# Layer 1's channel mixer on single PSUM banks, with an early copy of the first half product

## The chip, the cores and the metric

One NeuronCore of a Trainium2 chip runs one whole inference step of a small decoder. The metric is the time of one execution on the device in microseconds; before the change it is 2571.55 us, the median of three runs (2570.28 to 2572.80). Names of engines as in the profile: PE (TensorE matmul) and PEld (its weight loads), DVE (VectorE), ACT (ScalarE), POOL (GpSimd), SP (SyncE, which issues the DMAs). L521 is line 521 of the kernel.

## What is computed

Two layers over 1024 prompt tokens and 64 sample tokens, 1024 channels each. After every token mixer comes a channel mixer of 2816 hidden channels; the change touches layer 1's.

```python
def swiglu(h, w_in, w_out):
    g, u = jnp.split(h @ w_in, 2, axis=-1)
    return (jax.nn.silu(g) * u) @ w_out
...
        for layer in range(DEPTH):
            ...
            h = h + mix
            h = h + swiglu(rms_norm(h, norm_ffn_g[layer]), w_ffn_in[layer], w_ffn_out[layer])
        y = rms_norm(h, norm_final_g)
```

## The kernel before

**Data and groups.** Activations lie transposed, channels on partitions and tokens on the free axis. The 1088 tokens are two groups: GA, tokens 0 to 511, and GB, the 576 others. Layer 1's channel mixer runs first for GA, then for GB (`channel1`, which calls `run_ffn`).

**Precision.** Each float32 matmul is three matmuls of split operands: ACT casts a weight or activation to its high part, POOL (for weights, L186 and L197) or DVE (for activations, L241) subtracts to get the low part. Weights arrive by DMA into `stage` tiles (four buffers), and `w_split` turns them into `hl` tiles (three buffers). `w_next` takes the next `hl` tile, and splits two tiles ahead of it; so the call stands in the program where that work enters the queues of DVE, ACT and POOL. Every engine works off its queue in program order (the schedule is written by hand).

**Seven products for eight.** A block f of 128 hidden channels needs a gate part and an up part, each of 1024 input channels over the group's tokens. `strassen(f)` forms both from seven half products (half of the input channels by half of the tokens, 12 matmuls each) with sums of the weights and of the activations. The activations' sums (t1 to t4, b11, b21, b22) are formed once per group. The weights' sums are formed anew for every f on DVE: L200, L201 and L202 (`sum512`, and the two halves of `sum1024`) ahead of an f, L214 (`sum_c`) within it. The products are, in order: two halves of X, two of Y (the second is the "fourth product"), two of Z, and W. In the profile, "b" and "x" name the activation sums: an f is 36 matmuls on x, 12 on b, 12 on x, 24 on b, and the last 12 of these are W.

**From products to the gate.** ACT copies Y's second half into G (L537), since DVE adds one PSUM operand to one SBUF operand. DVE then adds: U's first half is X's first half plus G; U's second half is X's second half plus U's first; two sums of Y's first half go to P and G; three more take Z and W (all L525, seven per f). Then SiLU on ACT (L550), the gating product on POOL (L500) and the split for the next stage (L240 on ACT, L241 on DVE), the latter two deferred by `post`, `late` and `flush`.

**Order and stages.** The f are taken in pairs; after each pair but the first, the out blocks of the pair before follow: 8 blocks of 128 output channels, 12 matmuls each, added to the residual by DVE (L295). So the sums for an odd f enter DVE's queue in the even f, in the `w_next` that belongs to Z, ahead of that f's adds; the sums for the next even f are interleaved with the out blocks (`thin`). GA's last two pairs' out blocks come together at its end (`out_both`), where DVE also builds GB's operands. GB's f 0 is computed plainly.

**PSUM.** `accs()` takes a tile from a pool of three tiles of two banks each (`acc_pool(GB, 3)`), for both groups; two more banks serve small matmuls. In GA every tile but X, Y and Z uses half of its space. A tile is given out again when all readers of its last use are done. Hence W takes the tile that X had. Layer 0's second group uses `strassen` too, with `done` false (its activations aren't normalised beforehand in the same way); in layer 1 `done` is true.

Of the kernel before, what the change touches and what calls it, by code (L numbers as in the profile page):

```python
# [11 lines left out]
AF = mybir.ActivationFunctionType  # L12
# [33 lines left out]
GA = Grp(0, HALF, (0, 1, 512, 0))  # L46
GB = Grp(HALF, T, (0, 2, 288, 0))
# [10 lines left out]
def trunk_kernel(ctx, tc, x_prompt, x_sample, cache_k, cache_v, state_conformer, state_shortconv, state_pool,  # L58
# [4 lines left out]
    pe, act, dve, pool, sp = nc.tensor, nc.scalar, nc.vector, nc.gpsimd, nc.sync  # L63
# [12 lines left out]
    tmpbox = [gstack.enter_context(tc.tile_pool(name="tmpg", bufs=4, side="right")), 640]  # L76

    def tmp():
        return tmpbox[0].tile([128, tmpbox[1]], F, name="tmp")
# [89 lines left out]
    def need(upto):  # L169
        a, b, _ = seq[min(upto, len(seq)) - 1]  # L170
        return max(a, b or 0) + 1
# [50 lines left out]
    def w_next(live=0):  # L222
        j = wj[0]
        wj[0] += 1
        w_split(j + 3 - live)
        w_load(need(j + 6 - live))
        return hls.pop(j)
# [228 lines left out]
    def run_ffn(g, accs, ps, hidp, x, last, sig=False, slot=lambda: None, forms=None, plain=NF,  # L456
                free=lambda: None, hw=None, both=True):
        G = NF // 2
        n = g.n
        hid = {}  # L460
        gate = {}
        done = forms and "switch" not in forms

        def ev_g(a):
            t = tmp()
            if done:
                for p, o in parts(g, a, t):
                    act.activation(o, p, AF.Silu)
                gate["t"] = t
                return  # L470
            scaled(g, t[:, :n], a)
            if sig:
                s = tmp()
                act.activation(s[:, :n], t[:, :n], AF.Sigmoid)
                pool.tensor_tensor(t[:, :n], t[:, :n], s[:, :n], op=OP.mult)
            else:
                act.activation(t[:, :n], t[:, :n], AF.Silu)  # L477
            gate["t"] = t

        def to_hid(f):  # L480
            if f // 2 not in hid:
                hid[f // 2] = hidp.tile([128, 2, 2, hw or n], FR, name="hid")[:, :, :, :n]
            return hid[f // 2][:, f % 2]

        def ev_u(f, a):
            if done:
                t, dst = gate.pop("t"), to_hid(f)
                for p, o in parts(g, a, t):
                    dve.tensor_tensor(o, p, o, op=OP.mult)
                late.append(lambda: split(dst, t[:, :n]))  # L490
                return
            t = tmp()
            scaled(g, t[:, :n], a)
            gated(f, t, gate.pop("t"))

        def gated(f, t, u):
            dst = to_hid(f)

            def fin():
                (dve if both and f == NF - 1 else pool).tensor_tensor(t[:, :n], t[:, :n], u[:, :n], op=OP.mult)  # L500
                late.append(lambda: split(dst, t[:, :n]))
            post.append(fin)

        def one(f, which):
            h = w_next()
            a = accs()
            block(g, a, h, x, K0[4:] + K0[:4] if done else K0, slot=slot)
            flush()
            ev_g(a) if which == 0 else ev_u(f, a)
            slot()  # L510

        def strassen(f):
            w2 = n // 2

            def prod(acc, h, i, b):
                for k in range(4):
                    xk = forms[b](k)
                    for s, (wi, xi) in enumerate(((0, 0), (0, 1), (1, 0))):  # L520
                        pe.matmul(acc[:, :w2], h[:, wi, i, k], xk[:, xi], start=k == 0 and s == 0,  # L521
                                  stop=k == 3 and s == 2)

            def add(out, acc, x):
                dve.tensor_tensor(out, acc[:, :w2], x, op=OP.add)  # L525

            a, b = slice(0, w2), slice(w2, n)
            X, h = accs(), w_next()
            prod(X[:, 0], h, 0, "t2")
            prod(X[:, 1], h, 1, "t3")  # L530
            flush()
            slot()
            Y, h = accs(), w_next()
            prod(Y[:, 0], h, 0, "t1")
            prod(Y[:, 1], h, 1, "b11")
            G_, U, P = tmp(), tmp(), tmp()
            act.activation(G_[:, a], Y[:, 1, :w2], AF.Copy)  # L537
            Z, h = accs(), w_next()
            prod(Z[:, 0], h, 0, "t4")
            add(U[:, a], X[:, 0], G_[:, a])  # L540
            add(U[:, b], X[:, 1], U[:, a])
            add(P[:, b], Y[:, 0], U[:, b])
            add(G_[:, b], Y[:, 0], U[:, a])
            prod(Z[:, 1], h, 1, "b21")
            W, h = accs(), w_next()
            prod(W[:, 0], h, 0, "b22")
            add(P[:, a], Z[:, 0], U[:, b])
            add(G_[:, a], Z[:, 1], G_[:, a])
            add(G_[:, b], W[:, 0], G_[:, b])
            act.activation(G_[:, :n], G_[:, :n], AF.Silu)  # L550
            gated(f, P, G_)
            slot()

        for q in range(G + 1):
            if q < G:
                for f in (2 * q, 2 * q + 1):
                    if f >= plain:
                        if f == plain:
                            forms.get("switch", forms.get("ready"))()
                        strassen(f)  # L560
                        continue
                    if f == 0 and not done:
                        run_in(g, accs, x, [ev_g, lambda a: ev_u(0, a)], norm_hooks(g, ps, at=(4, 7)), skew=3)
                        slot()
                        continue
                    one(f, 0)
                    one(f, 1)
            if q == G - 1:
                free()
                if both:  # L570
                    return last([hid.pop(q - 1), hid.pop(q)])
            if q == G:
                flush()
                flush()
                last(hid.pop(q - 1))
            elif q:
                hh = hid.pop(q - 1)
                for o in range(2):
                    thin[0] = True
                    h = w_next()  # L580
                    thin[0] = False
                    for i in range(4):
                        a = accs()
                        out_block(g, a, h, i, hh)
                        added(g, hb[:, o * 4 + i, g.cs], a)
                        if parts_:
                            parts_.pop(0)()
                        if o == 0 and i == 1:
                            flush()
                        slot()  # L590
# [40 lines left out]
    def acc_pool(g, bufs):  # L631
        accstack.close()
        accbox["p"] = accstack.enter_context(tc.tile_pool(name=f"acc{g.c0}_{g.n}", bufs=bufs, space=PSUM))
        accbox["g"] = g

    def accs():
        return accbox["p"].tile([128, len(accbox["g"].blocks), 512], F, name="acc")
# [1087 lines left out]
    for n in range(2, KC):  # L1725
        h = w_next()
        a = accs()
# [4 lines left out]
    with tc.tile_pool(name="fab", bufs=1) as ep:  # L1732
        gen = forms_a(ep)
        for n in range(KC):
            h = w_next()
            a = accs()
# [8 lines left out]
    ystack0 = ExitStack()  # L1745
    tstack.close()
    r1stack.close()
    fp = fstack.enter_context(tc.tile_pool(name="forms1", bufs=1))
    tmpbox[:] = [ystack0.enter_context(tc.tile_pool(name="tmph", bufs=4, side="right")), 640]
    hidp1 = ystack0.enter_context(tc.tile_pool(name="hid1", bufs=2, side="right"))  # L1750
    xs = [fp.tile([128, 2 * GB.n], F, name=f"xs{k}") for k in range(4)]
    L, R = slice(0, W2), slice(W2, GB.n)
# [63 lines left out]
    def channel1(g, last, side, free, plain, x):  # L1816
        side = side()
        turn[0] = 0
        j0 = wj[0]

        def slot():
            turn[0] += 1
            if seam:
                return go_on()
            if jobs and g is GB:
                if turn[0] % 3 == 0:
                    jobs.pop(0)()
            elif turn[0] % 3 == 0:
                if g is GA or wj[0] > j0 + 2 * plain + 2:
                    next(side, 0)  # L1830

        def end(hh):
            if g is GB:
                for _ in side:
                    pass
                fstack.close()
            last(hh)

        run_ffn(g, accs, ms, hidp1, x, end, slot=slot, forms=dict(form_views(g.n // 2), ready=ready), plain=plain,
                free=free, hw=GB.n, both=g is GA)  # L1840
# [9 lines left out]
    def rows_a():  # L1850
# [11 lines left out]
        for t in range(4):  # L1862
            for i in range(2):
# [5 lines left out]
                sp.dma_start(y_p[0, t * 128:t * 128 + 128, 512 * i:512 * i + 512], y)  # L1869
                yield 1  # L1870

    channel1(GA, last_a1, forms_b, free_a, PLAIN1[0], None)


    ystack = ExitStack()
# [117 lines left out]
```

## Time and profile before

| | |
|---|---|
| median of three runs | 2571.55 us |
| the profiled execution | 2568.46 us |
| its span, first to last instruction | 2566.7 us |
| mean granted TensorE clock | 0.991 |
| GA's channel mixer of layer 1, about | 1774 to 2151 us of the span |
| GB's, without the final rows, about | 2151 to 2522 us |
| L537, copies of the fourth product | 60, 383 to 414 ns |
| L525, adds from PSUM | 420, 409 to 460 ns |

A row of the timeline reads: start, duration, engine, line, operation, output tile <- input tiles, shapes, how many were merged, and in brackets the idle time of the engine just before and what ended it. A row of waits reads: who waited, for whom, microseconds in all, how many times, the longest. A row of the stretches reads: its ends, its length, then the busy time of PE, PEld, DVE, ACT and POOL with the number of instructions, the granted clock, the DMA share and GB/s. Merged rows overlap where instructions are pipelined, so that a duration over a count is a little more than one's spacing.

### The profile page before, as it was taken

Reading aid. Unit: us, or ns where it says so; the run is one execution under the profiler, and the core shown is the slowest. Engines: PE = TensorE matmul, PEld = TensorE weight load, DVE = VectorE, ACT = ScalarE, POOL = GpSimd, SP = SyncE. Lnnn points to the kernel's source line nnn. Section 1 sums busy time; section 2 is a strip of 40 time slices with the busy share of each in tenths; the row PEclk is TensorE's granted clock in tenths of the full one; section 3 lists DMA queues with packets and bytes.
Section 4 is the critical chain, followed back from the end, with each engine's and each line's share of the span. In section 5 each row is a group of like instructions: output and inputs, shape, how many; then the busy total and the mean of one; then the engine's idle time right before and its main releaser. Section 6 shows DMA issues by size and latency. Waiting matters only on the chain.

```text
span 2566.7 us, 41423 instructions
## 1 busy us (share of the span) xinstructions
PE 2467.6 (96%) x15871; PEld 2196.0 (86%) x15871; DVE 1695.6 (66%) x2359; ACT 1106.1 (43%) x1875; POOL 1562.3 (61%) x1201
## 2 busy tenths in 40 slices
PE   8999999999999989999999999999999999999998
PEld 6788876777777768989999889989888888999997
DVE  3696767867878844567656633348777778666655
ACT  4536766754444334334333521234433444443333
POOL 6754234434443346678777722266888886887775
PEclk9999999999999999999999999999999999999999
DMA  7342231225455534222323411152323332333322
GB/s 220 114 113 74 65 105 50 62 66 158 143 171 166 148 108 156 70 74 83 99 83 99 129 42 42 44 158 61 92 85 97 99 99 83 107 95 103 99 84 79
DMA packets 355485, 258.31 MB, mean 101 GB/s; under 512 B 22913, under 2 KB 303617, under 8 KB 355272
## 3 DMA queue, kind: packets, MB, share of 16 engines
q1 hardware_dynamic: 355256, 255.66, 33.9%
q8 instruction: 126, 2.06, 0.3%
q14 instruction: 71, 0.58, 0.1%
q10 hardware_dynamic: 32, 0.01, 0.0%
HBM read 237.41 MB, written 18.69 MB: 100 GB/s over the span
## 4 chain that ended last, share of the span: by engine, by line
PE 45%; DVE 8%; POOL 2%; issue 1%; ACT 1%; POOLq 0%; DVEq 0%; ACTq 0%
PE acc L235 24%; PE acc L521 20%; POOL hl L197 1%; DVE hid L241 1%; DVE sum L200 1%; DVE sum L201 1%; DVE hb L295 1%; DVE b L1673 0%; DVE tmp L525 0%; DVE sum_c L214 0%; DVE sum L202 0%; DVE fb L1677 0%; PE blk L1896 0%; DVE x L1673 0%; POOL tmp L500 0%
## 5 line engine op out<-in xcount | busy, mean ns | idle before, releaser
L186 POOL TENSOR_TENSOR hl<-stage,hl 128x512 fp32r<-128x512 f32 x464 | 638.1, 1399 | 461.1 <-ACT hl L184 336.4
L235 PE MATMUL acc<-x,hl 128*128 128x512 f32 (+1 forms) x3648 | 788.4, 354 | 12.6 <-DVE hb L295 2.6
L235 PEld LDWEIGHTS acc<-x,hl 128*128 128x128 f32 x3648 | 584.8, 191 | 84.6 <-issue 14.1
L235 PE MATMUL acc<-hid,hl 128*128 128x288 f32 (+1 forms) x3096 | 551.3, 334 | 18.5 <-DVE hb L295 8.9
L235 PEld LDWEIGHTS acc<-hid,hl 128*128 128x128 f32 x3096 | 471.5, 190 | 72.4 <-DVE hb L295 13.0
L295 DVE TENSOR_TENSOR hb<-acc,hb 128x512 f32<-128x512 f32 (+1 forms) x360 | 256.1, 718 | 177.2 <-PE acc L235 175.8
L521 PE MATMUL acc<-x,hl 128*128 128x288 f32 (+1 forms) x2676 | 362.8, 291 | 4.7 <-POOL hl L197 1.9
L521 PEld LDWEIGHTS acc<-x,hl 128*128 128x128 f32 x2676 | 349.4, 189 | 7.1 <-POOL hl L197 2.7
L184 ACT ACTIVATE hl<-stage 128x1024 fp32r<-128x1024 f32 x232 | 243.6, 1055 | 224.0 <-PE acc L235 139.9
L197 POOL TENSOR_TENSOR hl<-sum,hl 128x512 fp32r<-128x512 f32 x180 | 237.1, 1345 | 168.5 <-ACT hl L196 168.5
L525 DVE TENSOR_TENSOR tmp<-acc,tmp 128x288 f32<-128x288 f32 (+1 forms) x420 | 173.5, 441 | 228.2 <-ACT tmp L537 135.4
L197 POOL TENSOR_TENSOR hl<-stage,hl 128x512 fp32r<-128x512 f32 x180 | 267.1, 1505 | 13.3 <-ACT hl L196 13.3
L521 PE MATMUL acc<-b,hl 128*128 128x256 f32 (+1 forms) x1548 | 216.6, 291 | 13.2 <-DVE tmp L525 10.3
L521 PEld LDWEIGHTS acc<-b,hl 128*128 128x128 f32 x1548 | 202.3, 190 | 18.8 <-ACT hl L196 8.5
L235 PE MATMUL acc<-x1t,hl 128*128 128x288 f32 x1152 | 216.4, 296 | 1.5 <-POOL hl L186 1.5
L235 PEld LDWEIGHTS acc<-x1t,hl 128*128 128x128 f32 x1152 | 196.1, 189 | 19.4 <-POOL hl L186 1.7
L196 ACT ACTIVATE hl<-sum 128x512 fp32r<-128x512 f32 x180 | 103.1, 623 | 237.2 <-DVE sum L202 212.3
L291 DVE TENSOR_TENSOR tmp<-acc,rr 128x512 f32<-128x512 f32 (+1 forms) x108 | 75.1, 709 | 111.1 <-PE acc L235 99.1
L500 POOL TENSOR_TENSOR tmp<-tmp 128x576 f32<-128x576 f32 (+1 forms) x85 | 127.6, 1501 | 16.3 <-ACT tmp L477 8.3
L196 ACT ACTIVATE hl<-stage 128x512 fp32r<-128x512 f32 x180 | 105.6, 618 | 67.3 <-PE acc L235 62.0
L241 DVE TENSOR_TENSOR hid<-tmp,hid 128x512 fp32r<-128x512 f32 (+1 forms) x88 | 100.0, 1138 | 48.1 <-ACT hid L240 47.8
L235 PE MATMUL acc<-x1a,hl 128*128 128x512 f32 x480 | 122.4, 409 | 3.0 <-POOL hl L186 1.3
(287 smaller groups left out, 3162.4 us busy)
## 6 DMA issues: line engine op xcount, KB each, us to landing
stage<-in_w_ffn_in_dram SPq DMA_DIRECT2D x176, 512.0 KB
stage<-in_w_ffn_out_dram SPq DMA_DIRECT2D x88, 512.0 KB
stage<-in_w_in_even_dram SPq DMA_DIRECT2D x40, 512.0 KB
kst<-in_cache_k_dram SPq DMA_DIRECT2D x64, 256.0 KB
vst<-in_cache_v_dram SPq DMA_DIRECT2D x64, 256.0 KB
stage<-in_w_out_even_dram SPq DMA_DIRECT2D x16, 512.0 KB
stage<-in_w_in_odd_dram SPq DMA_DIRECT2D x16, 512.0 KB
stage<-in_w_out_odd_dram SPq DMA_DIRECT2D x16, 512.0 KB
```

Of the source, the lines that this page charges most:

```text
L184: act.activation(hl[:, 0], st, AF.Copy)
L186: pool.tensor_tensor(hl[:, 1, c], st[:, c], f32(hl[:, 0, c]), op=OP.subtract)
L196: act.activation(hl[:, 0, c], x, AF.Copy)
L197: pool.tensor_tensor(hl[:, 1, c], x, f32(hl[:, 0, c]), op=OP.subtract)
L200: todo = [lambda: dve.tensor_tensor(sb, su[:, lo], su[:, hi], op=OP.add), lambda: dve.tensor_tensor(sa[:, hi], sg[:, lo], su[:, lo], op=OP ...
L235: pe.matmul(acc[:, b, :c1 - c0], w, xs[:, xi, c0 - o:c1 - o], start=first and s == 0, stop=last and s == 2)
L241: (on or dve).tensor_tensor(dst[:, 1], src, f32(dst[:, 0]), op=OP.subtract)
L291: dve.tensor_tensor(d, a, r, op=OP.mult)
L295: dve.tensor_tensor(d, a, d, op=OP.add)
L500: (dve if both and f == NF - 1 else pool).tensor_tensor(t[:, :n], t[:, :n], u[:, :n], op=OP.mult)
L521: pe.matmul(acc[:, :w2], h[:, wi, i, k], xk[:, xi], start=k == 0 and s == 0, stop=k == 3 and s == 2)
L525: dve.tensor_tensor(out, acc[:, :w2], x, op=OP.add)
```

## The change

In GA's layer 1 the pool becomes six tiles of one bank each (`acc_pool(GA, 6)`), and goes back to three pairs for GB. `bank()` hands out halves of a tile, so GB still works on pairs. In layer 1 (`done`) ACT copies X's first half into U right after that product, and the first add becomes Y's second half plus U, in place, placed right after the fourth product and so ahead of the `w_next` of Z. The copy of Y's second half into G stays, as G's first half is still needed later. The pool of temporaries gets a fifth buffer, as U is taken earlier.

```diff
+            box = []
+            def bank():
+                if not box:
+                    t = accs()
+                    box.extend(t[:, i] for i in range(t.shape[1]))
+                return box.pop(0)
...
-            X, h = accs(), w_next()
-            prod(X[:, 0], h, 0, "t2")
-            prod(X[:, 1], h, 1, "t3")
+            h = w_next()
+            X = bank(), bank()
+            prod(X[0], h, 0, "t2")
+            if done:
+                U = tmp()
+                act.activation(U[:, a], X[0][:, :w2], AF.Copy)
+            prod(X[1], h, 1, "t3")
             flush()
             slot()
...
-            prod(Y[:, 1], h, 1, "b11")
-            G_, U, P = tmp(), tmp(), tmp()
-            act.activation(G_[:, a], Y[:, 1, :w2], AF.Copy)
-            Z, h = accs(), w_next()
-            prod(Z[:, 0], h, 0, "t4")
-            add(U[:, a], X[:, 0], G_[:, a])
-            add(U[:, b], X[:, 1], U[:, a])
+            prod(Y[1], h, 1, "b11")
+            if done:
+                add(U[:, a], Y[1], U[:, a])
+            G_ = tmp()
+            act.activation(G_[:, a], Y[1][:, :w2], AF.Copy)
...
+            h = w_next()
+            Z = [bank()]
+            prod(Z[0], h, 0, "t4")
+            if not done:
+                add(U[:, a], X[0], G_[:, a])
+            add(U[:, b], X[1], U[:, a])
...
-            W, h = accs(), w_next()
-            prod(W[:, 0], h, 0, "b22")
+            h = w_next()
+            W = bank()
+            prod(W, h, 0, "b22")
...
-    tmpbox[:] = [ystack0.enter_context(tc.tile_pool(name="tmph", bufs=4, side="right")), 640]
+    tmpbox[:] = [ystack0.enter_context(tc.tile_pool(name="tmph", bufs=5, side="right")), 640]
...
+    acc_pool(GA, 6)
     channel1(GA, last_a1, forms_b, free_a, PLAIN1[0], None)
+    acc_pool(GB, 3)
```

How the queues change is best seen in one even f of GA, on DVE. Before (the rows from `sum_c` to the next `sum_c`; tile numbers follow the names, acc_19400 is X and acc_19434 is Y):

```order
L214 TENSOR_TENSOR sum_c_19402<-stage_19228,sum1024_19315 128x512 [waits DVE_49,Pool_49]
L241 TENSOR_TENSOR hid_19188<-tmp_19258,hid_19188 128x512 [waits Activation_49]
L200 TENSOR_TENSOR sum512_19469<-stage_19366 128x512 [waits DMAHW3_49,Pool_49]
L201 TENSOR_TENSOR sum1024_19468<-stage_19364,stage_19366 128x512 [waits DMAHW2_49,DVE_49]
L202 TENSOR_TENSOR sum1024_19468<-sum512_19469,stage_19364 128x512 [waits DVE_49]
L525 TENSOR_TENSOR tmp_19463<-acc_19400,tmp_19462 128x256 [waits Activation_49]
L525 TENSOR_TENSOR tmp_19463<-acc_19400,tmp_19463 128x256 [waits DVE_49]
L525 TENSOR_TENSOR tmp_19464<-acc_19434,tmp_19463 128x256 [waits DVE_49,PE_49]
```

And after (acc_19485 is the bank of Y's second half, acc_19452 that of X's second):

```order
L214 TENSOR_TENSOR sum_c_19445<-stage_19270,sum1024_19359 128x512 [waits DVE_49,Pool_49]
L241 TENSOR_TENSOR hid_19228<-tmp_19303,hid_19228 128x512 [waits Activation_49]
L525 TENSOR_TENSOR tmp_19465<-acc_19485,tmp_19465 128x256 [waits PE_49]
L200 TENSOR_TENSOR sum512_19516<-stage_19410 128x512 [waits DMAHW3_49,Pool_49]
L201 TENSOR_TENSOR sum1024_19515<-stage_19408,stage_19410 128x512 [waits DMAHW2_49,DVE_49]
L202 TENSOR_TENSOR sum1024_19515<-sum512_19516,stage_19408 128x512 [waits DVE_49]
L525 TENSOR_TENSOR tmp_19465<-acc_19452,tmp_19465 128x256
```

One add has moved ahead of the three sums and waits for PE alone, that is for the fourth product; the sums stand behind it.

On ACT, the same f before, from the hid cast to the cast of the sums:

```order
L240 ACTIVATE hid_19188<-tmp_19258 128x512 [waits Pool_49]
L196 ACTIVATE hl_19435<-sum_c_19402 128x512 [waits DVE_49,PE_49,Pool_49]
L537 ACTIVATE tmp_19462<-acc_19434 128x256 [waits PE_49]
L196 ACTIVATE hl_19467<-sum1024_19468 128x512 [waits DVE_49,Pool_49]
```

And after, where L541 is the new copy and L552 what was L537:

```order
L541 ACTIVATE tmp_19465<-acc_19451 128x256 [waits PE_49]
L240 ACTIVATE hid_19228<-tmp_19303 128x512 [waits Pool_49]
L196 ACTIVATE hl_19481<-sum_c_19445 128x512 [waits DVE_49,PE_49,Pool_49]
L552 ACTIVATE tmp_19511<-acc_19485 128x256 [waits DVE_49]
L196 ACTIVATE hl_19514<-sum1024_19515 128x512 [waits DVE_49,PE_49,Pool_49]
```

The new copy stands ahead of the hid cast, and the copy of the fourth product now waits for DVE (the add that reads the same bank) instead of PE.

On PE, the first matmul of W before (a tile of two banks) and after (one bank):

```order
L521 MATMUL acc_19505<-b2_0_16849,hl_19435 128x256 [waits DVE_49,Activation_49]
...
L521 MATMUL acc_19560<-b2_0_16849,hl_19481 128x256 [waits Activation_49]
```

W no longer waits for DVE there.

More of the change, by code (lines that the diff above doesn't have):

```diff
@@ L527, in strassen @@
             a, b = slice(0, w2), slice(w2, n)
-            X, h = accs(), w_next()
-            prod(X[:, 0], h, 0, "t2")
-            prod(X[:, 1], h, 1, "t3")
+            box = []
[11 more added lines that the diff above has]
+            prod(X[1], h, 1, "t3")
             flush()
             slot()
-            Y, h = accs(), w_next()
-            prod(Y[:, 0], h, 0, "t1")
-            prod(Y[:, 1], h, 1, "b11")
-            G_, U, P = tmp(), tmp(), tmp()
-            act.activation(G_[:, a], Y[:, 1, :w2], AF.Copy)
-            Z, h = accs(), w_next()
-            prod(Z[:, 0], h, 0, "t4")
-            add(U[:, a], X[:, 0], G_[:, a])
-            add(U[:, b], X[:, 1], U[:, a])
-            add(P[:, b], Y[:, 0], U[:, b])
-            add(G_[:, b], Y[:, 0], U[:, a])
-            prod(Z[:, 1], h, 1, "b21")
-            W, h = accs(), w_next()
-            prod(W[:, 0], h, 0, "b22")
-            add(P[:, a], Z[:, 0], U[:, b])
-            add(G_[:, a], Z[:, 1], G_[:, a])
-            add(G_[:, b], W[:, 0], G_[:, b])
+            h = w_next()
+            Y = bank(), bank()
+            prod(Y[0], h, 0, "t1")
+            prod(Y[1], h, 1, "b11")
[4 more added lines that the diff above has]
+            if not done:
+                U = tmp()
+            P = tmp()
+            h = w_next()
+            Z = [bank()]
+            prod(Z[0], h, 0, "t4")
+            if not done:
+                add(U[:, a], X[0], G_[:, a])
+            add(U[:, b], X[1], U[:, a])
+            add(P[:, b], Y[0], U[:, b])
+            add(G_[:, b], Y[0], U[:, a])
+            Z.append(bank())
+            prod(Z[1], h, 1, "b21")
+            h = w_next()
+            W = bank()
+            prod(W, h, 0, "b22")
+            add(P[:, a], Z[0], U[:, b])
+            add(G_[:, a], Z[1], G_[:, a])
+            add(G_[:, b], W, G_[:, b])
             act.activation(G_[:, :n], G_[:, :n], AF.Silu)
```

## The prediction

> **What bounds the kernel now.** I read the page's head first, then busy time in stretches, then PE's waits in the two stretches that the change touches, and last the timeline of one period there.
>
> ```profile
> PE 2467.6 (96%) x15871; PEld 2196.0 (86%) x15871; DVE 1695.6 (66%) x2359; ACT 1106.1 (43%) x1875; POOL 1562.3 (61%) x1201
> ...
> 1838.00:2102.00 264.00, 255.49 (x1728) 230.63 (x1727) 191.43 (x263) 103.54 (x176) 221.05 (x160) 1.00 0.33 96
> ...
> 2260.00:2522.00 262.00, 261.63 (x1973) 261.40 (x1972) 164.24 (x247) 101.18 (x166) 204.17 (x151) 1.00 0.34 100
> ```
>
> TensorE is the bound of the whole. In the first group's channel mixer (first stretch, to 2151 with its end) it idles 8.5 us of 264; in the second group's (last row) 0.4 us of 262. So nothing can be gained in the second group, only lost. In the first, over 1774 to 2151:
>
> ```profile
> PE acc L521 <- DVE tmp L525: 10.3, 12, 2.9
> PE acc L521 <- POOL hl L197: 3.8, 5, 1.7
> PE acc L235 <- DVE hb L295: 3.4, 3, 1.9
> ```
>
> The 10.3 us are the waits at W: its tile is X's, and X is free only when the adds on DVE have read it. Single banks aim at this and, in the out blocks, at the 3.4 us. What decides is what comes next behind those waits. One period (an even f, X at 1972.38, then the odd f):
>
> ```profile
> 1972.38 4.43 PE L521 MATMUL acc<-x,hl 128*128 128x256 f32 x36
> 1973.18 4.71 POOL L197 TENSOR_TENSOR hl<-stage,hl 128x512 fp32r<-128x512 f32 x3
> 1973.18 1.85 DVE L214 TENSOR_TENSOR sum_c<-stage,sum 128x512 f32<-128x512 f32 x1
> 1974.96 1.78 DVE L241 TENSOR_TENSOR hid<-tmp,hid 128x512 fp32r<-128x512 f32 x1
> 1976.66 1.78 DVE L200 TENSOR_TENSOR sum<-stage 128x512 f32<-128x512 f32 x1
> 1977.85 1.74 POOL L197 TENSOR_TENSOR hl<-sum_c,hl 128x512 fp32r<-128x512 f32 x1
> 1978.26 0.39 ACT L537 ACTIVATE tmp<-acc 128x256 f32<-128x256 f32 x1 [2.15 <-PE acc L521]
> 1978.36 1.77 DVE L201 TENSOR_TENSOR sum<-stage 128x512 f32<-128x512 f32 x1
> 1980.06 0.68 DVE L202 TENSOR_TENSOR sum<-sum,stage 128x512 f32<-128x512 f32 x1
> 1980.66 2.39 DVE L525 TENSOR_TENSOR tmp<-acc,tmp 128x256 f32<-128x256 f32 x6
> 1981.54 4.25 POOL L197 TENSOR_TENSOR hl<-sum,hl 128x512 fp32r<-128x512 f32 x3 [1.95 <-ACT hl L196]
> 1981.68 1.66 PE L521 MATMUL acc<-b,hl 128*128 128x256 f32 x12 [0.61 <-DVE tmp L525]
> ...
> 1985.75 3.78 POOL L197 TENSOR_TENSOR hl<-stage,hl 128x512 fp32r<-128x512 f32 x3
> 1989.29 1.05 ACT L184 ACTIVATE hl<-stage 128x1024 fp32r<-128x1024 f32 x1
> 1989.50 1.29 POOL L500 TENSOR_TENSOR tmp<-tmp 128x512 f32<-128x512 f32 x1
> 1990.76 1.28 POOL L197 TENSOR_TENSOR hl<-sum_c,hl 128x512 fp32r<-128x512 f32 x1
> 1992.10 1.24 PEld L521 LDWEIGHTS acc<-b,hl 128*128 128x128 f32 x10 [0.25 <-POOL hl L197]
> ```
>
> Two things are to be seen. From 1981.54 POOL runs without a gap (1981.54 + 4.25 is 1985.79, and so on to the out weights), and TensorE, 10 us behind its wait at the even W, waits for POOL at the odd one (1992.10). That chain starts when the weight sums for the next f (L200 to L202) are done at 1980.74: cast on ACT, then POOL at +0.8. So **the binding chain is sums on DVE, then POOL; the W wait lies beside it**. And a sum or a split is slow only when DVE and POOL run at once: L200 takes 1.78 beside POOL and L202 0.68 with POOL idle, and a POOL split 1.74 against 1.28. The excess is the other's instruction: they take turns.
>
> **The change part by part.** Removed: the waits of W on the adds. W now takes the bank of the first half of X, which ACT copies as soon as it is written. By the rows W would start 0.6 us earlier, or 0.8 with the overlap of matmuls that TensorE also loses there. Added: 43 ACT copies of 0.39 to 0.41 us (row L537), some 17 us on an engine that is busy 104 of 264 us. Behind each in ACT's queue stands the hid cast that feeds L241; the copy ends near 1974.4 and the cast at 1975.0, where L241 begins now: 0, with nothing to spare. ACT's old copy of the fourth product now waits for the add, as both read that bank: 0.4 us later. Behind it stand the weight sums' casts, which wait for DVE longer, or in the odd f the casts of the out weights (L184, 1989.29), whose POOL half isn't reached before 1992.04: 0, covered by 1.7 us.
>
> At nothing I cost further the fifth tmp buffer, the second swap of pools, and the first swap: X's first bank is then the one that the layer's last out block left, so that TensorE starts about 1 us later, but in the first f it loses the like to POOL anyway (most of the 3.8 us above); without that cover it costs 1 us. The number of DMAs and SP's order stay, and so does layer 0, where the new branch isn't taken.
>
> Moved: the first of the adds, to ahead of the three sums in DVE's queue. It must wait for the fourth product (Y's second half: the time at which L537 starts). In each f whose successor follows without out blocks, L200 to L202 now stand behind that wait; L200 began 1.6 us before it at 1978.26. This is the price, and by taking turns it is worked out so:
>
> *First group, nine periods with out blocks.* Add from 1978.26 to 1978.65. Without L200 in between, POOL's third split ends at 1977.9 and the sum_c split at about 1979.15 (1.28). L200 waits for that and ends 0.54 later, 1979.7; L201 0.6 more, L202 0.68 more: 1980.9 against 1980.74. So +0.15 each; the binding chain passes it on, and the 0.8 us at W become waits for POOL at the next X and the odd W. 9 x 0.15 = **+1.4 us**.
>
> *First group, start (f 0 to 3).* No outs lie between f 1 and f 2, and POOL is loaded when the sums come:
>
> ```profile
> 1807.07 1.79 DVE L200 TENSOR_TENSOR sum<-stage 128x512 f32<-128x512 f32 x1
> 1809.85 0.39 ACT L537 ACTIVATE tmp<-acc 128x256 f32<-128x256 f32 x1 [2.15 <-PE acc L521]
> 1809.97 1.74 POOL L500 TENSOR_TENSOR tmp<-tmp 128x512 f32<-128x512 f32 x1
> 1810.48 1.78 DVE L202 TENSOR_TENSOR sum<-sum,stage 128x512 f32<-128x512 f32 x1
> ```
>
> Here L202 ends at 1812.26. With L200 held until the fourth product is there, about 1809 (now 1809.85; TensorE arrives 0.8 us earlier here, because the norm's 2.9 us stall at W goes), three turns with POOL end it near 1813.1, and the POOL chain behind it by as much: **+1.0 us** for the start.
>
> *First group, end.* TensorE stalls 1.85 us in the last out blocks because DVE builds the second group's operands; with six banks it doesn't. But those operands set when the second group can go on, so I count only the idle time of DVE in that stretch, which an earlier TensorE fills:
>
> ```profile
> 2145.17 6.02 PE L235 MATMUL acc<-hid,hl 128*128 128x512 f32 x18 [1.85 <-DVE hb L295]
> ...
> 2149.82 0.69 DVE L295 TENSOR_TENSOR hb<-acc,hb 128x512 f32<-128x512 f32 x1 [0.61 <-PE acc L235]
> ...
> 2151.23 0.69 DVE L295 TENSOR_TENSOR hb<-acc,hb 128x512 f32<-128x512 f32 x1 [0.35 <-PE acc L235]
> ```
>
> 0.61 + 0.35: **-1.0 us**.
>
> *Second group, f 2 (and f 4, f 6).* Its tiles are still pairs of banks, so W waits for the add that reads X's second half, and this add now comes after the sums.
>
> ```profile
> 2178.73 1.78 DVE L200 TENSOR_TENSOR sum<-stage 128x512 f32<-128x512 f32 x1
> 2182.13 1.77 DVE L202 TENSOR_TENSOR sum<-sum,stage 128x512 f32<-128x512 f32 x1
> 2184.51 3.59 PE L521 MATMUL acc<-b,hl 128*128 128x288 f32 x24
> ...
> 2215.86 1.79 DVE L200 TENSOR_TENSOR sum<-stage 128x512 f32<-128x512 f32 x1
> 2218.68 0.41 ACT L537 ACTIVATE tmp<-acc 128x288 f32<-128x288 f32 x1 [2.50 <-PE acc L521]
> 2219.27 1.78 DVE L202 TENSOR_TENSOR sum<-sum,stage 128x512 f32<-128x512 f32 x1
> ```
>
> In f 2 L200 moves from 2178.73 to 2183.3, meets the gating product and one split, and L202 ends near 2187.5, not 2183.9. The add to U's second half follows at 2187.9; W, due at 2186.1, starts at 2188: **+1.7 us** after what it waits now. In f 4, L202 ends at 2222.6 instead of 2221.05 by the same count, W starts 1.0 later; f 6 (2252.59 on) is alike: **+2.0 us**.
>
> *Second group, the rest.* The sums are late too, but POOL is idle then:
>
> ```profile
> 2328.14 1.74 POOL L197 TENSOR_TENSOR hl<-sum_c,hl 128x512 fp32r<-128x512 f32 x1
> 2330.30 0.41 ACT L537 ACTIVATE tmp<-acc 128x288 f32<-128x288 f32 x1 [2.50 <-PE acc L521]
> 2331.70 3.34 PE L521 MATMUL acc<-b,hl 128*128 128x288 f32 x24
> ```
>
> Add 2330.30, L200 from 2330.67, L201 and L202 0.6 apart, done at 2332.55; the next add ends at 2332.93, and W is due at 2333.3 (half of the 3.34 us). 0.2 us of slack: **0**, and no more than that stands between it and seven further stalls.
>
> All of this rests on two prices, that of a turn and that of an add from PSUM, which takes none (lowest, median and highest in ns):
>
> ```profile
> L525 DVE TENSOR_TENSOR tmp<-acc,tmp x420: 409/448/460, 1152.4 to 2522.7; 128x288 f32<-128x288 f32 x89, 128x256 f32<-128x256 f32 x51
> ```
>
> The Trainium skill (SBUF — State Buffer, "Who interferes with whom") says that a DVE instruction with two SBUF inputs and a GpSimd instruction that reads SBUF hold one port in turn, each for its whole length, and that one SBUF input doesn't contend. By that rule, the trace agrees, the late sums are short where POOL is idle. Were L200 and L201 slow by nature (1.78 us each anywhere), each of some 20 f's would end its sums 2.2 us later, and the sum would be up to 44 us worse.
>
> Sum: 1.4 + 1.0 - 1.0 + 1.7 + 2.0 = **+5.1 us**. The profiled execution took 2568.46 us, so 2573.6 by it; on the median of the runs shown, 2571.55, that is **2576.6**.
>
> **The rivals.** *The stalls pay (0.15).* If POOL has slack that the timeline doesn't show, or less contention speeds it, the 10.3 us at W and the 3.4 us in the out blocks come back for the most part: -10 in the first group, with the second's +3.7: 2565. For it: POOL idles 1.95 us a period ahead of the sums. Against it: that gap waits for the sums, which move the wrong way. *Nothing moves (0.20).* The sums slip in between POOL's splits as early as now, and the loaded f's lose nothing: 0 +- 2, 2572. *The second group's slack is gone (0.20).* If the sums end 0.5 us later than I work out (one turn with POOL in the steady periods), W waits 0.3 to 1.0 us in seven more f's: +2 to +7 beyond the forecast, 2579 to 2584; it decides once the add to U's second half ends after 2333.1. *The forecast (0.45):* 2573 to 2580.
>
> **How the numbers follow.** 0.2% is 5.1 us, about what a measurement of this kernel can tell from no change. Faster: most of the first rival, 0.13. Slower: the third and half of the forecast, 0.42. The rest, 0.45, is within. The range from 2566 to 2584 leaves out most of the first rival and the tail of the third. The first group alone has bounds of -10.3 (all of W's waits) and +12 x 2.0 if no turn is won.
>
> **What would show it.** Right: no waits of TensorE on L525 in the first group, more on L197 instead; periods of 32.5 to 32.8 us there; L202 ending 0.1 to 0.3 us later against X; in the second group, waits on L525 at f 2, 4 and 6. Wrong: periods below 32.2 us (POOL wasn't the bound), or waits on L525 in all of the second group (the slack was less).

## The result, and the profile after

The changed kernel takes 2594.31 us (median of 4 runs, 2591.85 to 2599.22) beside 2570.91 us for the one before (4 runs): a ratio of 1.0095, 95% interval 1.0079 to 1.0110, so **23.4 us slower**, far above the forecast of 2576.6 and outside its range. The profiled execution took 2595.99 us with a span of 2594.2, against 2568.46 and 2566.7.

The page's first line of busy times, after:

```profile
PE 2476.5 (95%) x15871; PEld 2199.1 (85%) x15871; DVE 1648.6 (64%) x2359; ACT 1118.4 (43%) x1918; POOL 1546.6 (60%) x1201
```

And the two stretches shown of before (the ends are the same, so they hold the work a little shifted):

```profile
1838.00:2102.00 264.00, 255.66 (x1718) 230.29 (x1716) 168.59 (x258) 106.02 (x189) 218.01 (x160) 1.00 0.32 95
...
2260.00:2522.00 262.00, 251.08 (x1866) 247.61 (x1865) 149.03 (x236) 99.97 (x171) 185.66 (x142) 1.00 0.31 93
```

In GA TensorE is as busy as before (255.7 us against 255.5). In GB, where it had 0.4 us of idle time, it now has 10.9 us in 262. TensorE's waits of the changed kernel from 1774 to 2551 say for what (for whom, us in all, times, the longest):

```profile
PE acc L521 <- ACT tmp L541: 17.0, 21, 1.5
PE acc L521 <- POOL hl L197: 12.2, 20, 1.6
PE acc L235 <- DVE hb L295: 3.4, 1, 3.4
PE acc L521 <- ACT hl L196: 2.8, 4, 1.6
...
PE acc L521 <- DVE tmp L525: 0.3, 1, 0.3
```

In GA the waits at W on L525 are gone, and those on POOL have grown in their place, as forecast. But the largest row is one that the prediction doesn't have: 17.0 us, once in each of GB's 21 seven-product f, on L541, the new copy.

To see where the time lies I divided the layer at the starts of X in the timeline. The table holds all kernels of this study (us, to about 0.1, each from one profile); the last column is the median beside that of the kernel before, run in the same session.

| kernel | GA f 0 to f 4 | GA f 4 to f 20 | GA f 20 to GB f 1 | GB f 1 to f 20 | median, us (before) |
|---|---|---|---|---|---|
| before | 63.7 | 264.4 | 61.3 | 336.4 | |
| the change | 64.8 | 267.0 | 64.6 | 353.1 | 2594.31 (2570.91) |
| e1 GB as before | 64.9 | 266.9 | 63.0 | 334.9 | 2574.78 (2570.19) |
| e2 copy behind X | 64.8 | 267.6 | 64.2 | 338.3 | 2576.23 (2570.19) |
| e3 sums first | 62.3 | 262.4 | 62.7 | 352.6 | 2588.89 (2570.19) |
| e4 banks alone | 62.6 | 262.9 | 62.7 | 335.0 | 2566.45 (2570.19) |
| e5 e4 + banks shifted | 62.6 | 263.0 | 62.7 | 335.0 | 2565.75 (2568.94) |
| e6 e4 + gate on DVE | 61.5 | 257.9 | 61.6 | 335.1 | 2560.74 (2568.94) |
| e7 change mended | 62.3 | 262.5 | 62.7 | 336.2 | 2564.59 (2568.94) |
| e8 e4 + early sums | 62.6 | 256.3 | 61.7 | 335.0 | 2557.19 (2568.94) |
| e9 pairs + early sums | 65.2 | 259.2 | 60.6 | 336.5 | 2564.86 (2571.42) |
| e10 e9 + gate on DVE | 65.5 | 253.5 | 60.3 | 336.7 | 2559.34 (2571.42) |
| e11 e8 + gate on DVE | 62.4 | 252.1 | 59.7 | 336.5 | 2553.56 (2571.42) |
| e12 before + swap | 65.2 | 264.1 | 61.2 | 336.4 | 2571.68, one run (2571.42) |

The first and third columns scatter: e12 is the kernel before up to GA's end, and takes 65.2 us to f 4 beside 63.7; the change and e1 have the same GA, and take 64.6 and 63.0 us in the third. So 1.5 us there, between two single profiles, can't be told from nothing.

The change's 27.5 us by the profiles are 1.1 + 2.6 + 3.3 in GA, 16.7 in GB to f 20 and 2.1 behind it, and 1.7 ahead of GA's first X, of which 0.9 us is a wait for the last add (L295) before it. The other 0.8 is scatter: this start lies between 1769 and 1780 us in these profiles, whatever the kernel.

**GB.** The timeline of the changed kernel shows the wait, in an even f and in an odd one:

```profile
2339.35 1.75 PE L521 MATMUL acc<-x,hl 128*128 128x288 f32 x12
2341.14 0.41 ACT L541 ACTIVATE tmp<-acc 128x288 f32<-128x288 f32 x1 [0.30 <-PE acc L521]
2341.60 3.46 PE L521 MATMUL acc<-x,hl 128*128 128x288 f32 x24 [0.50 <-ACT tmp L541]
...
2426.07 1.75 PE L521 MATMUL acc<-x,hl 128*128 128x288 f32 x12
2428.39 0.39 ACT L541 ACTIVATE tmp<-acc 128x288 f32<-128x288 f32 x1
2428.84 3.46 PE L521 MATMUL acc<-x,hl 128*128 128x288 f32 x24 [1.01 <-ACT tmp L541]
```

X's first half is 12 matmuls; then TensorE stands still until ACT has copied it, and only then writes the second half. In the odd f ACT still has weight casts ahead of the copy. From start to start it takes 2.25 and 2.77 us where 12 matmuls of an unbroken row take 1.6: some 1.8 us in a pair of f. Before, the 36 matmuls of X and of Y's first half were one row:

```profile
2359.75 4.96 PE L521 MATMUL acc<-x,hl 128*128 128x288 f32 x36
```

GB's X is one tile of two banks, and the program orders a write behind every earlier read of the same tile. The copy stands between the two halves, so the second half waits for a read of the first. GA's halves are two tiles, and there the same copy runs beside TensorE (ACT at 2043.37 within the unbroken 36):

```profile
2041.77 4.38 PE L521 MATMUL acc<-x,hl 128*128 128x256 f32 x36
2043.37 0.38 ACT L541 ACTIVATE tmp<-acc 128x256 f32<-128x256 f32 x1
...
2047.36 1.31 POOL L197 TENSOR_TENSOR hl<-sum_c,hl 128x512 fp32r<-128x512 f32 x1
2047.60 0.42 DVE L525 TENSOR_TENSOR tmp<-acc,tmp 128x256 f32<-128x256 f32 x1 [2.60 <-PE acc L521]
2047.94 1.27 DVE L200 TENSOR_TENSOR sum<-stage 128x512 f32<-128x512 f32 x1
2049.74 0.68 DVE L202 TENSOR_TENSOR sum<-sum,stage 128x512 f32<-128x512 f32 x1
```

The Trainium skill (PSUM — Partial Sum Buffer, "PSUM bank collisions raise a hardware error") says that two engines collide within one bank (in the same partitions), not across different ones. These rows agree: the copy reads one bank while TensorE writes another. So the wait in GB is the program's and not the chip's.

**GA's periods.** The rows above are one period. The sums end (L202) at 2050.42, that is 8.65 us after X; before it was 8.36, the forecast had 8.52. In about every second period it is worse, since POOL's split of sum_c starts later and collides with L201:

```profile
2014.78 1.74 POOL L197 TENSOR_TENSOR hl<-sum_c,hl 128x512 fp32r<-128x512 f32 x1
2015.29 1.78 DVE L201 TENSOR_TENSOR sum<-stage 128x512 f32<-128x512 f32 x1
2016.99 0.68 DVE L202 TENSOR_TENSOR sum<-sum,stage 128x512 f32<-128x512 f32 x1
```

There X starts at 2008.43 and the sums end 9.24 us later. The periods are 32.75 us for the first kind and 33.34 for the second: 24.1 us after the sums' end in both, and 24.2 before (32.53 - 8.36).

### The profile page after: what moved, and what is told of

Read it like the earlier page. It is cut to its first block, busy times and chain, and to the rows that moved or that the text cites. A ratio compares the mean times of both kernels' runs of the same rounds, so it can differ in the third digit from the quotient of the medians.

```text
span 2594.2 us, 41416 instructions
## 1 busy us (share of the span) xinstructions
PE 2476.5 (95%) x15871; PEld 2199.1 (85%) x15871; DVE 1648.6 (64%) x2359; ACT 1118.4 (43%) x1918; POOL 1546.6 (60%) x1201
## 5 line engine op out<-in xcount | busy, mean ns | idle before, releaser
L186 POOL TENSOR_TENSOR hl<-stage,hl 128x512 fp32r<-128x512 f32 x464 | 638.4, 1402 | 459.9 <-ACT hl L184 336.5
L235 PEld LDWEIGHTS acc<-hid,hl 128*128 128x128 f32 x3096 | 470.9, 189 | 65.2 <-DVE hb L295 7.5
L521 PE MATMUL acc<-x,hl 128*128 128x288 f32 (+1 forms) x2676 | 375.2, 293 | 31.8 <-ACT tmp L541 17.0
L521 PEld LDWEIGHTS acc<-x,hl 128*128 128x128 f32 x2676 | 352.0, 189 | 44.3 <-ACT tmp L541 21.9
L295 DVE TENSOR_TENSOR hb<-acc,hb 128x512 f32<-128x512 f32 (+1 forms) x360 | 254.9, 717 | 174.0 <-PE acc L235 172.9
L525 DVE TENSOR_TENSOR tmp<-acc,tmp 128x288 f32<-128x288 f32 (+1 forms) x420 | 171.9, 440 | 292.5 <-PE acc L521 238.7
L184 ACT ACTIVATE hl<-stage 128x1024 fp32r<-128x1024 f32 x232 | 243.5, 1055 | 213.3 <-PE acc L235 140.0
L197 POOL TENSOR_TENSOR hl<-stage,hl 128x512 fp32r<-128x512 f32 x180 | 256.1, 1446 | 13.1 <-ACT hl L196 13.0
```

Of the source, the lines that this page charges most:

```text
L184: act.activation(hl[:, 0], st, AF.Copy)
L186: pool.tensor_tensor(hl[:, 1, c], st[:, c], f32(hl[:, 0, c]), op=OP.subtract)
L197: pool.tensor_tensor(hl[:, 1, c], x, f32(hl[:, 0, c]), op=OP.subtract)
L235: pe.matmul(acc[:, b, :c1 - c0], w, xs[:, xi, c0 - o:c1 - o], start=first and s == 0, stop=last and s == 2)
L295: dve.tensor_tensor(d, a, d, op=OP.add)
```

## The experiments

**e1.** The four places in `strassen` that ask for `done` ask for GA as well; the first of them:

```diff
+            early_u = done and g is GA
...
-            if done:
+            if early_u:
                 U = tmp()
                 act.activation(U[:, a], X[0][:, :w2], AF.Copy)
```

> GA as in the change, GB with the arithmetic of before (no early copy, no moved add). Theory T (in GB TensorE's second half of X waits for ACT's copy of the first half, since both are one tile; 17.0 us of waits): GB takes from its f 1 to its end what it took before, so about 18.7 us less than the change: 2575 to 2577. Rival R1 (GB is slower because the weight sums come late, as my forecast had it, or because of the fifth temporary buffer or the pool): with the buffer or the pool to blame it stays above 2585; the sums alone can't be told from T here, that is the next run's part.

Measured: 2574.78 us, ratio 1.0019 (1.0009 to 1.0029). GB takes 334.9 us. The fifth buffer and the pool cost GB nothing.

**e2.** Only the place of the copy is changed.

```diff
-            if done:
-                U = tmp()
-                act.activation(U[:, a], X[0][:, :w2], AF.Copy)
             prod(X[1], h, 1, "t3")
+            if done:
+                U = tmp()
+                act.activation(U[:, a], X[0][:, :w2], AF.Copy)
```

> The early copy is placed behind the second half of X; ACT's order is the same, and GA, where the halves are two tiles, changes nowhere. Theory T: the second half of X has nothing to wait for, the 21 waits on L541 (17.0 us) are gone, and what stays of GB's loss is that of the moved add, forecast at 3.7 us: 2577 to 2581. Rival R1 (the late sums cost GB its 18.7 us): waits on L541 turn into waits on L525 or L197, 2590 or more.

Measured: 2576.23 us, ratio 1.0027 (1.0018 to 1.0037). The waits on L541 are gone, X is one row again, and of TensorE's waits in GB this is what is left of weight; below it X in the timeline of e2:

```profile
PE acc L521 <- DVE tmp L525: 3.4, 3, 1.5
```

```profile
2367.70 4.96 PE L521 MATMUL acc<-x,hl 128*128 128x288 f32 x36
```

Three waits, 3.4 us, and 338.3 us for GB against 334.9 in e1: the moved add costs GB 3.4 us. The copy between the two writes costs 353.1 - 338.3 = 14.8 us to f 20, and 2.1 in the last pair. **The theory of the shared tile is shown.**

**e3.** The add stands behind `w_next` again.

```diff
-            if done:
-                add(U[:, a], Y[1], U[:, a])
...
             prod(Z[0], h, 0, "t4")
+            if done:
+                add(U[:, a], Y[1], U[:, a])
```

> The first add is placed behind the three weight sums again (after the first half of Z), the early copy stays where the change has it. GB keeps its waits on L541. Theory S (in GA the sums on DVE lead POOL's chain, and the moved add delays them): GA's periods go from 33.2 back to about 32.5 us or less and the first four f lose about 1 us less, 2590 to 2592 in all, with fewer waits on L197. Rival R2 (the moved add costs nothing; GA's loss is the early copy on ACT or the pool): GA's periods as in the change, 2593 to 2596.

Measured: 2588.89 us, ratio 1.0077 (1.0064 to 1.0091). GA's periods fall to 32.37 to 32.40 us and its start by 2.5 us: the moved add costs GA 64.8 + 267.0 - 62.3 - 262.4 = 7.1 us there. One period of e3, X at 2034.65:

```profile
2037.81 1.78 DVE L200 TENSOR_TENSOR sum<-stage 128x512 f32<-128x512 f32 x1
...
2041.21 1.78 DVE L202 TENSOR_TENSOR sum<-sum,stage 128x512 f32<-128x512 f32 x1
```

The sums begin earlier, are slow beside POOL, and still end at X + 8.34.

**e4.** The pool of six single banks with the old arithmetic in both groups (the new branch never taken).

> Single banks for GA and the old arithmetic in both groups. Theory S (POOL's chain binds GA's periods, and the pool's two swaps cost at GA's start and end): W's waits on L525 become waits on L197 at the same period, GA's start and end lose 1.7 and about 3 us as in the change, GB nothing: 2574 to 2577. Rival R3 (W's waits were the bound): up to 10 us less than before, 2561 to 2568. Rival R4 (the swaps cost nothing by themselves): 2570 to 2572.

Measured: 2566.45 us, ratio 0.9990 (0.9980 to 1.0001): 3.7 us less by the medians, not told from no change. All of W's waits are gone, and the period falls only from 32.53 to 32.35. TensorE's waits between GA's f 4 and f 20, before and in e4:

```profile
PE acc L521 <- DVE tmp L525: 5.6, 8, 1.3
```

```profile
PE acc L522 <- POOL hl L197: 4.5, 10, 0.9
```

The first wait has turned into the second. The total lies where R3 had it, but not for R3's reason, which would have shown in the periods: from f 4 to f 20 the banks bring 1.5 us. The rest is the start, which gains 1.1 us where I had a loss (2.6 beside e12's start), GB, which finds its operands ready (1.4), and an end that loses 1.4 and not 3.

**e5.** Four tiles are handed out unused, so that GA's last out blocks stand in other banks.

```diff
     acc_pool(GA, 6)
+    for _ in range(4):
+        accs()
```

> As the run with the banks alone, but four tiles of the pool of six are handed out unused at GA's start. GA takes 22 x 7 + 88 = 242 tiles, two more than a multiple of six, so its last two out blocks stand in the very banks that GB's first pair gets; shifted by four they stand in the last two. Theory P (the swap of pools costs at GA's end because the first pair waits for the last out block's add): the 3.4 us wait of TensorE on L295 before GB's first product goes, and the slow clock behind it; from the last pair's X to that of GB's f 1 it takes 62.7 us now and 58.5 to 60.5 then; in all 2 to 4 us less than with the banks alone. Rival R5 (DVE's work for GB's operands sets that stretch): the wait moves to the operands, and the stretch stays at 62 to 63 us.

Measured: 2565.75 us, ratio 0.9990 (0.9981 to 0.9999); every stretch is that of e4, and the 3.4 us wait on L295 stays. P falls: it isn't the place of the last blocks. But the wait is on that add and not on the operands, so R5 doesn't hold either; e12 takes it up.

**e6.** GA's gating product goes to DVE.

```diff
-                (dve if both and f == NF - 1 else pool).tensor_tensor(t[:, :n], t[:, :n], u[:, :n], op=OP.mult)
+                (dve if both and (done or f == NF - 1) else pool).tensor_tensor(t[:, :n], t[:, :n], u[:, :n], op=OP.mult)
```

> As the run with the banks alone, but in GA the gating product (L500, two a period, 1.3 to 1.75 us each) goes from POOL to DVE. It stands behind the sums in POOL's chain, ahead of the split that the odd W waits for. Theory S1 (POOL's work behind the sums sets GA's period): the period falls by 1.0 to 1.4 us to about 31.2, 8 to 11 us in all. Theory S2 (the end of the sums on DVE sets it, 24.1 us before the next pair's X in every version; POOL behind it only adds the 0.3 us at the odd W): 32.0 to 32.4, no more than 3 us in all.

Measured: 2560.74 us, ratio 0.9965 (0.9951 to 0.9979). The period is 31.83: 0.5 us less than e4's, between the two theories, and so is the whole, some 5 us less. The sums end at X + 8.20, hardly earlier than e4's X + 8.31; most of the rest is what TensorE waited for POOL behind the sums (from f 4 to f 20, 1.9 us where e4 has 4.5). So POOL's work behind the sums counts too.

**e7.** e2 and e3 together: the change with both places mended.

> The change with both places mended: the early copy behind the second half of X, the first add behind the weight sums. Theory: GB takes what it took before (about 335 us from f 1 to the last pair), GA's periods 32.4, so the whole is like the banks alone: 2565 to 2569; the early copy itself, 43 more copies on ACT, neither costs nor gains. Rival: the early copy costs something of its own, on ACT or by the adds' order: 2571 or more.

Measured: 2564.59 us, ratio 0.9982 (0.9973 to 0.9992), by stretches within 1.2 us of e4. Beyond that, the early copy by itself neither costs nor gains.

**e8.** On e4: DVE forms the next odd f's sums (L200 to L202) right behind `sum_c`, where no out blocks come between; the casts and splits stay in `w_next`.

```diff
             prod(X[1], h, 1, "t3")
+            if done and g is GA:
+                sums_ahead()
```

> As the run with the banks alone, but in GA the three weight sums for the next odd f stand on DVE right behind sum_c (L214), ahead of the split of hid (L241); casts and splits stay where they are. Theory S2: the sums end at about X + 6.8 us in place of X + 8.3, POOL's first split of them begins at X + 7.8 in place of X + 9.1, and GA's period falls by 1.0 to 1.4 us, to 31.0 to 31.4 us, where TensorE has no idle time left: 9 to 12 us less than with the banks alone, 2554 to 2558. Theory S1 (POOL's amount of work sets the period): POOL's splits come earlier but contend more with DVE, the period stays at 32.2 or more. Rival R6 (the split of hid comes too late for the out blocks): a new wait of TensorE on L241, no gain.

Measured: 2557.19 us, ratio 0.9957 (0.9944 to 0.9971); periods of 31.42 to 31.46 us. One period of e8, X at 2025.2 (L184 to L186 are the three sums there, L211 the split):

```profile
2026.61 1.78 DVE L184 TENSOR_TENSOR sum<-stage 128x512 f32<-128x512 f32 x1
...
2030.01 1.78 DVE L186 TENSOR_TENSOR sum<-sum,stage 128x512 f32<-128x512 f32 x1
...
2031.20 1.74 POOL L211 TENSOR_TENSOR hl<-sum_c,hl 128x512 fp32r<-128x512 f32 x1
2032.91 4.25 POOL L211 TENSOR_TENSOR hl<-sum,hl 128x512 fp32r<-128x512 f32 x3
2035.10 4.39 PE L539 MATMUL acc<-x,hl 128*128 128x256 f32 x36
```

The sums end at X + 6.6, POOL goes from the split of sum_c straight to theirs, and the odd X starts 9.9 us after the even one without a wait. **When the sums are ready sets more of the period than how much POOL does**: 0.9 us here, 0.5 in e6. It isn't all: the sums are ready 1.7 us earlier, but POOL, still at the split of sum_c, begins theirs only 1.4 us earlier (X + 7.7 for 9.1). TensorE's waits from f 4 to f 20 are down to this:

```profile
PE acc L539 <- POOL hl L211: 1.6, 3, 0.6
```

**e9.** The early sums alone, on the kernel before (pairs of banks).

> The kernel before (pairs of banks, no early copy, no swap of pools) with one edit: in GA the weight sums for the next odd f stand right behind sum_c on DVE. Theory S2 (the sums' end sets GA's period): period near 31.4 us as with single banks and early sums, because the adds that W waits for are also free earlier; no wait on L295 at GA's start (0.9 us) and at GB's first product (3.4 us): 2553 to 2558, at least as good as with single banks. Rival R7 (single banks are needed too): W's waits on L525 stay, 0.5 us or more each, the period is 32 us or more, 2562 to 2566.

Measured: 2564.86 us, ratio 0.9969 (0.9956 to 0.9982); periods of 31.9 us. The gain is about half of what I expected, and R7 holds in part: W waits for the adds again, 10.6 us over GA, 5.9 of them once at the start. With the sums early the single banks are worth 0.5 us a period; without that they were worth 0.2. (At the start they are worth 2.6 us here, and as much without the early sums, by e12's start and e4's.)

**e10 and e11.** The gating product on DVE as in e6, on e9 (pairs) and on e8 (single banks).

> The run before it, with GA's gating product on DVE in place of POOL as well. If what is left of POOL's chain still costs: the period falls by another 0.2 to 0.4 us to about 31.1, 2 to 4 us less. If TensorE is the bound by then: same within 1 us.

> Single banks, early sums and the gating product on DVE, to be set beside the run before it: the same periods, and 1 to 3 us more in all, which are the waits at the two swaps of pools (0.9 and 3.4 us, less the 1.85 us stall in the last out blocks that the pairs have).

Measured: 2559.34 us, ratio 0.9949 (0.9936 to 0.9962), periods 31.22; and 2553.56 us, ratio 0.9927 (0.9914 to 0.9940), periods 31.13 to 31.25. e10 takes 5.5 us off e9, and 0.7 off the period, where I had 2 to 4 and 0.2 to 0.4: POOL's work counted for more with pairs than I had it. I had e11 behind e10, for the swaps of pools; it is 5.8 us ahead, since GA's start is 3.1 us shorter with single banks and the swaps cost little. In e11 TensorE waits for nothing from f 4 to f 20. **It beats both kernels**: 17.9 us less than before.

**e12.** The kernel before, with `acc_pool(GB, 3)` once more between the groups.

> The kernel before with one needless edit: the pool of three pairs is closed and opened again between GA and GB. Theory P2 (a new pool's first tile waits until all tiles of the old pool are free, wherever they stand): TensorE's first product of GB, which now starts at 2151.03 with the last out block's add (L295, 2151.23) still to come, starts behind that add, about 0.9 us or more later, with a wait on L295 there that the kernel before doesn't have. Rival P (only the tile in the same banks counts): no such wait, since the pairs' order puts another block there, the same time.

Measured: 2571.68 us, in one run. The last out block's add and GB's first product, in e12:

```profile
2152.75 0.68 DVE L295 TENSOR_TENSOR hb<-acc,hb 128x512 f32<-128x512 f32 x1
2153.58 3.55 PE L235 MATMUL acc<-b,hl 128*128 128x288 f32 x25 [1.27 <-DVE hb L295]
```

GB's first product, which before starts ahead of the last add, now starts behind it. P2 holds: the first tile of a new pool waits for all of the old one. Here the 1.27 us didn't show in the stretch (61.2), since TensorE ran at the full clock in it, and before it didn't (last section).

## Why the prediction was wrong

**The step that failed** is the one on what was added: "Added: 43 ACT copies [...] 0, with nothing to spare." I followed the copy along ACT's queue, asked what stands behind it there, and never asked who has to wait for the copy itself. In GB it is read and write of one tile, and TensorE waits: 16.9 of the 27.5 us. The prediction used this very rule for W in GB ("Its tiles are still pairs of banks, so W waits for the add"), and not for X's second half. The listing of the order couldn't tell it: the first matmul of X's second half reads "waits Activation" before and after, first for a weight cast long done, now for the copy. The code could have: `bank()` hands out halves of one tile in GB, and the copy stands between two `prod` calls that write them. The price was there too: a copy of 0.41 us behind a product, 21 times, while TensorE has 0.4 us of idle time. That alone is 8.6 us, some half of what was lost; in the odd f ACT has weight casts ahead of the copy as well.

**GA's periods:** right in mechanism, too small. The waits at W were beside the chain and turned into waits on POOL (e4), so the first rival, 2565, was wrong for the change. The moved add delays the sums, and the period follows. I had 8 x 0.15 = 1.2 us between f 4 and f 20, and 2.6 were measured, the net of 4.6 for the moved add and 2.0 that the banks bring (e3). The error is in the turns: I worked out one order of sums and split, and about every second period has another, 0.6 us worse. The chain that I named, sums on DVE and then POOL, holds in both its parts: the period falls by 0.9 us with the sums earlier (e8), by 0.5 with less work for POOL (e6), by 1.2 with both (e11).

**GA's start:** +1.0 forecast, +1.1 measured, but by luck: the moved add costs 2.5 us (e3) and the banks bring 1.1 (e4), not the near nothing that I had. Beside e12's start it would be -0.4, and the banks would bring 2.6. The wait at the first swap of pools, costed at nothing, is 0.9 us.

**GA's end:** -1.0 forecast, +3.3 measured. The 1.85 us stall in the out blocks went, as forecast, and what came late next was not the operands but GB's first tile, which a new pool gives out only after the last add: 3.4 us, that is 1.5 us more than the stall before. The moved add is another 0.9 us (the out blocks behind the last pair begin 21.9 us after its X, not 21.0; 21.4 in e1, with the same GA). The rest, about 1 us, is the clock (below): e1's end, with less of it, is +1.7.

**GB's adds:** +3.7 forecast for f 2, 4 and 6 and 0 for the others; e2 against e1 shows three waits and 3.4 us, none of the seven further stalls. This term, and the slack of 0.2 us that it rested on, held.

So e2, the change without the one oversight, measures 2576.23 us where I forecast 2576.6. That is partly chance: GA lost about 7 us in it where I had 1.4.

## What to carry to other kernels

When an instruction is put between two writes of one tile, ask what the tile is: a program that tracks tiles makes the second write wait for a read of the first, even in another bank, and an engine with no idle time pays it every time. Put such a read behind the last write, or make the halves tiles of their own. And a wait of the busiest engine that lies beside the binding chain is worth nothing until that chain is shorter: the same single banks brought 0.2 us a period at first, and 0.5 once the sums came early.

## What was not expected of the hardware

After the 3.4 us stall at GA's end TensorE ran slowly for a while, but not always. Here is, of the changed kernel, the timeline's row of the first 25 matmuls, and the stretch that holds them (the granted clock is the third number from its end):

```profile
2157.17 6.17 PE L235 MATMUL acc<-b,hl 128*128 128x288 f32 x25 [3.39 <-DVE hb L295]
```

```profile
2157.00:2163.50 6.50, 6.33 (x28) 6.36 (x29) 6.43 (x11) 0.91 (x2) 3.11 (x3) 0.54 0.27 81
```

And of e11, after a stall as long:

```profile
2141.23 3.55 PE L252 MATMUL acc<-b,hl 128*128 128x288 f32 x25 [3.40 <-DVE hb L312]
```

```profile
2142.00:2148.00 6.00, 6.00 (x48) 6.00 (x47) 5.93 (x9) 1.15 (x2) 2.68 (x3) 1.00 0.31 89
```

The same 25 matmuls take 6.17 us at 0.54 and 3.55 at 1.00, a difference of 2.6 us by the clock alone; in e4 they take 5.08. Before, it was 0.72 behind the 1.85 us stall, and in e12 1.00 behind a stall of the same length. The Trainium skill (TensorE: Matmul & The Clock Gate, "Part 1: The HAM clock gate") says that an idle window of about 3.4 us halves the clock, and that the window runs freely. The traces agree on the half and on the length: in them the granted clock is 1.00 or 0.50 around these stalls, and the slow stretches last 3.41 or 6.83 us. But the window need not be idle as a whole. These rows are such windows, laid out from the ends of the slow stretches, of TensorE alone: ends, length, its busy time, the clock, then DMA. First the changed kernel, then the one before, then e11, whose window ends follow from its last slow stretch at 1808.47:

```profile
2152.74:2156.15 3.41, 1.04 (x5) 1.00 0.01 2
2156.15:2159.56 3.41, 2.39 (x10) 0.50 0.00 0
2159.56:2162.98 3.42, 3.42 (x16) 0.50 0.49 147
2162.98:2166.39 3.41, 3.41 (x28) 1.00 0.04 11
```

```profile
2142.42:2145.83 3.41, 1.56 (x7) 1.00 0.45 135
2145.83:2149.25 3.42, 3.42 (x10) 0.50 0.00 0
```

```profile
2136.15:2139.56 3.41, 1.68 (x8) 1.00 0.00 0
2139.56:2142.98 3.42, 1.75 (x13) 1.00 0.00 0
2142.98:2146.39 3.41, 3.41 (x28) 1.00 0.27 76
```

Before, the whole stall of 1.85 us falls into one window, which is busy for 1.56 us, and the next window runs at half the clock. In e11 the longer stall spreads over two windows, 1.73 us idle in one and 1.67 in the other, and the clock stays. The 14 profiles, from 1700 to 2530 us, agree: every full-clock window with 1.76 us of idle time or more (23 of them) is followed by one at half the clock, and none with 1.73 or less is. So in these runs about half a window of idle time was enough, and whether a stall of 1.8 to 3.4 us costs anything further depends on where it falls. A difference of 2 us in a stretch with such a stall is not the kernel's.
